# Feed-forward of a two-layer decoder trunk: two of the four weight sums of each seven-product step made by accumulating transfers, the others in place, with plain half steps between the products

## The chip, the cores and the metric

One core of a Trainium2 chip runs the whole program. The metric is the device time of one execution in microseconds. Below, PE is the matrix engine, PEld its weight loads, DVE the vector engine, ACT the scalar engine, POOL the GpSimd engine, and SP the engine that issues the transfers.

## The reference

A trunk of two layers over 256 tokens of width 2048, all in 32-bit floats. Layer 0 mixes by a gated position-wise block beside cross-attention into 256 memory tokens; layer 1 mixes by multi-head latent attention beside the same kind of cross-attention. What matters here is the channel mixer that ends each layer, with D_FF = 5632:

```
def swiglu_ffn(h, w_gate, w_up, w_down):
    return (jax.nn.silu(h @ w_gate) * (h @ w_up)) @ w_down

h = h + rms_norm(mix, norm_gains[i, 1])
f = swiglu_ffn(rms_norm(h, norm_gains[i, 2]), ffn_w_gate[i], ffn_w_up[i], ffn_w_down[i])
h = h + rms_norm(f, norm_gains[i, 3])
```

## The kernel before

**Number format.** Each 32-bit operand is split into two parts of a shorter format, `hi` and `lo`, and a product becomes three matmuls: hi by hi, hi by lo, lo by hi (`mm3`, L212 to L214). Activations are split once and kept. Weights are streamed: a transfer of the SP queue brings them into a staging tile `wst` (three in a ring), ACT casts to `whi` (L166 in `split`, L179 in `wsplit`), DVE subtracts to get `wlo` (L167, L181). `whi` and `wlo` are rings of four, so a split may run at most four groups of matmuls ahead of PE.

**The feed-forward.** The weights of gate and up lie interleaved, 256 columns of gate and then 256 of up. `ffn` goes through the hidden columns in five parts (`parts`), of 2, 2, 2, 2 and 3 chunks of 1024 columns. After each part `to_tokens` multiplies what the part made by the rows of `w_down` that belong to it. The first part is all plain matmuls. In parts two to five, so in nine chunks of a layer and 18 in all, a chunk has four steps `g`, each over a quarter of the 16 feature tiles, and a step has two halves:

- `seven_step` on one half of the chunk's columns treats tokens, features and gate/up as 2 by 2 blocks and makes seven block products in the place of eight. It needs the four loaded weight blocks (b11 and b21 are gate, b12 and b22 are up), and four sums of them. Its products go to four PSUM banks, the set `seven`.
- `plain_step` on the other half makes the ordinary products in 512-column matmuls, 24 of them, into two banks of the set `other`.

There are 72 steps. In a step a seven-product half has 7 products of 2 tiles by 3 matmuls, 42 matmuls of 256 columns.

**The sums before.** `stage` loads both halves with two 512 KB transfers each into `wst` tiles. In `seven_step` DVE makes two sums at once (L504, 1024 columns, reading `wst` and writing a separate tile `ws`), then the third (L508) and the fourth (L510), 512 columns each. ACT and DVE split the pair b11, b21, the pair of sums one and three, the pair two and four, and b22 alone. After the last step of a chunk `seven_hidden` puts the seven products together and applies the gate, while the plain half of that step is still to come; then `hidden` does the same for the plain half.

**What sets the order.** The code emits instructions in program order, small background pieces (`tick`, `to_features`) in between; a scheduler then fixes one static order for every engine's queue from tiles, buffers and its own estimates. On the chip each queue runs strictly in that order. Nothing runs on POOL in the feed-forward.

Of the kernel before, what the change touches and what calls it, by code (L numbers as in the profile page):

```python
# [10 lines left out]
F32 = mybir.dt.float32  # L11
# [6 lines left out]
P = 128  # L18
# [30 lines left out]
def trunk(ctx, tc, x, mem, positions, norm_gains, w_mem_kv, w_down, a_w_in, a_b_s, a_w_out, w_kv_a, w_uk, w_uv,  # L49
# [352 lines left out]
    def ffn(i, xp, r, R, gcol, each, hp, need):  # L402
# [66 lines left out]
        def stage(col, g):  # L469

            st = wtile().rearrange("p (h k n) -> p h k n", h=2, k=2)
            rows = w_gate_up[i].rearrange("(h k p) n -> p h k n", h=2, p=P)
            for e in range(2):
                sp.dma_start(out=st[:, e], in_=rows[:, e, 2 * g:2 * g + 2, col:col + 512])
            return st

        def parts_of_sum(src, n=1024):
            hi = wpool.tile([P, 1024], F32R, tag="whi", name="whi", bufs=4)
            lo = wpool.tile([P, 1024], F32R, tag="wlo", name="wlo", bufs=4)
            hv, lv = hi[:, :n], lo[:, :n]  # L480
            if len(src.shape) == 4:
                hv, lv = [t.rearrange("p (h k n) -> p h k n", h=2, k=2) for t in (hv, lv)]
            elif len(src.shape) == 3:
                hv, lv = [t.rearrange("p (k n) -> p k n", k=2) for t in (hv, lv)]
            split(hv, lv, src)
            return hi, lo

        def seven_step(col, g, X):
            st = stage(col, g)
            room = tmp.tile([P, D], F32, tag="gb", name="ws", bufs=2)  # L490
            t13, t24 = room[:, :1024], room[:, 1024:]
            b11, b21, b22 = st[:, 0, :, :S], st[:, 1, :, :S], st[:, 1, :, S:]
            sums = room.rearrange("p (s k n) -> p s k n", s=4, k=2)
# [21 lines left out]

        def seven_hidden(X, f):

            m1, m2, m5, m6 = X[0][:, :S], X[0][:, S:], X[1][:, S:], X[3][:, :S]
            v = tmp.tile([P, 512], F32, tag="lat", name="v", bufs=2)
            act.copy(out=v[:, :S], in_=m1)  # L520
            dve.tensor_tensor(out=v[:, S:], in0=m6, in1=v[:, :S], op=ALU.add)
            u = tmp.tile([P, 512], F32, tag="lat", name="u", bufs=2)
            dve.tensor_tensor(out=u.rearrange("p (x n) -> p x n", x=2), in0=X[1].rearrange("p (x n) -> p x n", x=2),
                              in1=v[:, S:].rearrange("p (o n) -> p o n", o=1).broadcast_to([P, 2, S]), op=ALU.add)
            dve.tensor_tensor(out=m1, in0=m2, in1=v[:, :S], op=ALU.add)
            sg = tmp.tile([P, 512], F32, tag="sg", name="sg")
            act.activation(out=sg[:, :S], in_=m1, func=AF.Silu)
            dve.tensor_tensor(out=X[2], in0=X[2], in1=u, op=ALU.add)
            act.activation(out=sg[:, S:], in_=X[2][:, :S], func=AF.Silu)
# [29 lines left out]
        for pi, (c0, ncn) in enumerate(parts):  # L559
# [572 lines left out]
```

## Time and profile before

| | |
|---|---|
| median of 3 runs | 2120.69 us (2119.86 to 2126.76) |
| profiled execution | 2121.68 us, span of the trace 2120.0 us |
| PE, PEld | 2094.3 us busy (99%), 1835.1 us (87%) |
| DVE, ACT, POOL | 1568.0 us (74%), 1119.4 us (53%), 4.1 us (0%) |
| granted PE clock | 0.998 of full |
| DMA | 397.05 MB on SP's queue, 188 GB/s over the span |
| weight transfers of the feed-forward, up and gate | 288 of 512 KB, 4.5 us from issue to landing (median) |

Busy shares are averages over stages with different limits; the stretches of the trace in which seven-product steps run are eight, one for each part but the first of either layer. A row that says "idle 1.19 <-ACT whi L166" means that the engine stood idle 1.19 us before this instruction and that the ACT instruction at L166 which writes `whi` ended the wait. Matmuls overlap in the record, so their rate is read from the distance of their starts.

### The profile page before, as it was taken

Reading aid. Unit: us, or ns where it says so; the run is one execution under the profiler, and the core shown is the slowest. Engines: PE = TensorE matmul, PEld = TensorE weight load, DVE = VectorE, ACT = ScalarE, POOL = GpSimd, SP = SyncE. Lnnn points to the kernel's source line nnn. Section 1 sums busy time; section 2 is a strip of 40 time slices with the busy share of each in tenths; the row PEclk is TensorE's granted clock in tenths of the full one; section 3 lists DMA queues with packets and bytes.
Section 4 is the critical chain, followed back from the end, with each engine's and each line's share of the span. In section 5 each row is a group of like instructions: output and inputs, shape, how many; then the busy total and the mean of one; then the engine's idle time right before and its main releaser. Section 6 shows DMA issues by size and latency. Waiting matters only on the chain.

```text
span 2120.0 us, 30041 instructions
## 1 busy us (share of the span) xinstructions
PE 2094.3 (99%) x11922; PEld 1835.1 (87%) x11922; DVE 1568.0 (74%) x2151; ACT 1119.4 (53%) x1478; POOL 4.1 (0%) x11
## 2 busy tenths in 40 slices
PE   8999999999999999999999999999999999999998
PEld 7889989788888888889889998978888888889987
DVE  6556755976868878689767775597686877868966
ACT  6544444655545545455545654565554554545543
POOL 0000000000000000000000000000000000000000
PEclk9999999999999999999999999999999999999999
DMA  9655365555565655655754534555556565565563
GB/s 359 250 181 174 92 221 185 178 181 177 195 202 179 201 179 186 209 178 199 242 176 136 181 122 140 183 174 189 177 190 200 178 218 179 189 207 168 199 222 130
DMA packets 153981, 398.96 MB, mean 188 GB/s; under 512 B 9456, under 2 KB 16880, under 8 KB 152816
## 3 DMA queue, kind: packets, MB, share of 16 engines
q1 hardware_dynamic: 153840, 397.05, 56.4%
q8 instruction: 93, 1.52, 0.3%
q14 instruction: 48, 0.39, 0.1%
HBM read 394.91 MB, written 2.10 MB: 187 GB/s over the span
## 4 chain that ended last, share of the span: by engine, by line
PE 91%; DVE 5%; DMA 2%; ACT 1%; issue 1%; SPq 0%; DVEq 0%; ACTq 0%
PE bank L214 29%; PE bank L213 29%; PE bank L212 29%; DMA wst<-in_w_gate_up 2%; PE bank L418 1%; DVE wlo L181 1%; DVE wlo L187 1%; DVE h L362 1%; PE bank L240 0%; PE bank L1016 0%; PE bank L1017 0%; DVE ws L504 0%; PE bank L707 0%; PE bank L1041 0%; DVE wlo L167 0%
## 5 line engine op out<-in xcount | busy, mean ns | idle before, releaser
L212 PE MATMUL bank<-whi,hl 128*128 128x512 f32 (+3 forms) x2880 | 1030.8, 359 | 0.9 <-ACT hl L166 0.7
L213 PE MATMUL bank<-wlo,hl 128*128 128x512 f32 (+3 forms) x2880 | 1026.6, 356 | 3.6 <-DVE wlo L181 1.9
L214 PE MATMUL bank<-whi,hl 128*128 128x512 f32 (+3 forms) x2880 | 1025.5, 356 | 0.0
L181 DVE TENSOR_TENSOR wlo<-wst,whi 128x1024 fp32r<-128x1024 f32 (+1 forms) x398 | 468.8, 1183 | 237.5 <-ACT whi L179 236.2
L213 PEld LDWEIGHTS bank<-wlo,hl 128*128 128x128 f32 x2880 | 542.3, 188 | 82.1 <-DVE wlo L181 4.1
L214 PEld LDWEIGHTS bank<-whi,hl 128*128 128x128 f32 x2880 | 542.3, 188 | 77.6 <-DVE hl L167 0.5
L212 PEld LDWEIGHTS bank<-whi,hl 128*128 128x128 f32 x2880 | 542.5, 188 | 76.2 <-ACT hl L166 1.9
L179 ACT CAST whi<-wst 128x1024 fp32r<-128x1024 f32 (+1 forms) x398 | 405.0, 1020 | 381.2 <-PE bank L214 346.3
L187 DVE SCALAR_TENSOR_TENSOR wlo<-wst,gains,whi 128x1024 fp32r<-128x1024 f32 (+3 forms) x216 | 255.7, 1193 | 131.0 <-ACT whi L185 128.1
L185 ACT ACTIVATE whi<-wst,gains 128x1024 fp32r<-128x1024 f32 (+3 forms) x216 | 232.2, 1080 | 216.7 <-PE bank L214 131.2
L166 ACT CAST whi<-ws 128x1024 fp32r<-128x1024 f32 x144 | 151.1, 1049 | 159.0 <-PE bank L214 81.0
L167 DVE TENSOR_TENSOR wlo<-ws,whi 128x1024 fp32r<-128x1024 f32 x144 | 175.6, 1220 | 57.0 <-ACT whi L166 56.8
L166 ACT CAST whi<-wst 128x1024 fp32r<-128x1024 f32 (+1 forms) x144 | 120.3, 835 | 108.1 <-PE bank L214 107.3
L167 DVE TENSOR_TENSOR wlo<-wst,whi 128x1024 fp32r<-128x1024 f32 (+1 forms) x144 | 137.0, 951 | 22.0 <-ACT whi L166 22.0
L212 PE MATMUL bank<-hl,whi 128*128 128x256 f32 x448 | 129.1, 288 | 7.0 <-ACT whi L185 7.0
L214 PE MATMUL bank<-hl,wlo 128*128 128x256 f32 x448 | 127.1, 285 | 1.0 <-DVE wlo L187 1.0
L213 PE MATMUL bank<-hl,whi 128*128 128x256 f32 x448 | 127.1, 284 | 0.0
L504 DVE TENSOR_TENSOR ws<-wst 128x1024 f32<-128x1024 f32 x72 | 88.0, 1223 | 26.1 <-DMA wst<-in_w_gate_up 25.7
L212 PEld LDWEIGHTS bank<-hl,whi 128*128 128x128 f32 x448 | 85.2, 190 | 10.2 <-ACT whi L185 7.0
L213 PEld LDWEIGHTS bank<-hl,whi 128*128 128x128 f32 x448 | 85.2, 190 | 2.8
L214 PEld LDWEIGHTS bank<-hl,wlo 128*128 128x128 f32 x448 | 84.8, 190 | 1.5 <-DVE wlo L187 1.4
L213 PE MATMUL bank<-wlo,sx 128*128 128x256 f32 x288 | 81.2, 282 | 0.0
(206 smaller groups left out, 1549.7 us busy)
## 6 DMA issues: line engine op xcount, KB each, us to landing
wst<-in_w_gate_up SPq DMA_DIRECT2D x288, 512.0 KB, 4.5
wst<-in_ffn_w_down SPq DMA_DIRECT2D x76, 1024.0 KB, 5.1
wst<-in_w_gate_up SPq DMA_DIRECT2D x32, 1024.0 KB, 4.9
wst<-in_a_w_in SPq DMA_DIRECT2D x24, 1024.0 KB, 5.1
wst<-in_w_mem_kv SPq DMA_DIRECT2D x15, 1024.0 KB, 6.5
wst<-in_ffn_w_down SPq DMA_DIRECT2D x12, 768.0 KB, 4.5
wst<-in_a_w_out SPq DMA_DIRECT2D x8, 1024.0 KB, 6.0
wst<-in_b_w_in SPq DMA_DIRECT2D x8, 1024.0 KB, 4.9
```

What stands on the lines that cost most here:

```text
L166: ins = act.copy(out=hi, in_=src)
L167: dve.tensor_tensor(out=lo, in0=src, in1=hi.bitcast(F32), op=ALU.subtract)
L179: act.copy(out=hi[:, :n], in_=src)
L181: dve.tensor_tensor(out=lo[:, :n], in0=src, in1=hi[:, :n].bitcast(F32), op=ALU.subtract)
L185: act.activation(out=hi[:, :n], in_=src, func=AF.Copy, scale=g)
L187: dve.scalar_tensor_tensor(out=lo[:, :n], in0=src, scalar=g, in1=hi[:, :n].bitcast(F32), op0=ALU.mult, op1=ALU.subtract)
L212: pe.matmul(out=o, lhsT=a[0], rhs=b[0], start=start, stop=False, **kw)
L213: pe.matmul(out=o, lhsT=a[0], rhs=b[1], start=False, stop=False, **kw)
L214: line["pe"] = pe.matmul(out=o, lhsT=a[1], rhs=b[0], start=False, stop=stop, **kw).ins
L362: ins = dve.scalar_tensor_tensor(out=h[:, b, cs], in0=yv, scalar=rs[b], in1=h[:, b, cs], op0=ALU.mult, op1=ALU.add)
L418: pe.transpose(out=pt[:, q, b, :], in_=hv[:, b * S + q * P:b * S + (q + 1) * P], identity=ident)
L504: dve.tensor_tensor(out=sums[:, 0:2], in0=st[:, :, :, S:], in1=st[:, 0].rearrange("p k (x n) -> p x k n", x=2), op=ALU.add)
```

## The change

The step's own weights get a tile of their own, `ws`, of four blocks q0 to q3 (256 KB each; the ring of two that held the sums before). SP loads b11, b21, b22 and once more b11 into q0 to q3, 256 columns wide each. Two sums are made by transfers that POOL issues and that add what they read to what lies in SBUF: b12 onto q3 as soon as b11 has landed there, and b12 onto q2 (which holds b22) once b22 has been split. DVE makes the other two in place: q0 = q2 + q0, then q1 = q0 + q1. The products are put into four groups in another order, and the two plain halves of a step stand ahead of the first and between the second and the third. The plain half now takes the first 512 columns of a chunk and the seven products the second, so `seven_hidden` comes last in a chunk.

```
-        def stage(col, g):
-
-            st = wtile().rearrange("p (h k n) -> p h k n", h=2, k=2)
-            rows = w_gate_up[i].rearrange("(h k p) n -> p h k n", h=2, p=P)
-            for e in range(2):
-                sp.dma_start(out=st[:, e], in_=rows[:, e, 2 * g:2 * g + 2, col:col + 512])
-            return st
...
+        def seven_step(col, g, X, between):
+
+            st = tmp.tile([P, D], F32, tag="gb", name="ws", bufs=2)
+            q = st.rearrange("p (q k n) -> p q k n", q=4, k=2)
+            own = rows[:, :, 2 * g:2 * g + 2, :]
+            gate, up = slice(col, col + S), slice(col + S, col + 2 * S)
+            for to, e, c in ((0, 0, gate), (1, 1, gate), (2, 1, up), (3, 0, gate)):
+                sp.dma_start(out=q[:, to], in_=own[:, e, :, c])
+            pool_e.dma_start(out=q[:, 3], in_=own[:, 0, :, up], accum_op=ALU.add)
...
-            wt = parts_of_sum(st[:, :, :, :S])
-            dve.tensor_tensor(out=sums[:, 0:2], in0=st[:, :, :, S:], in1=st[:, 0].rearrange("p k (x n) -> p x k n", x=2),
-                              op=ALU.add)
+            front, back = st[:, :1024], st[:, 1024:]
+            wt = own_split(front)
             products(wt, (xp, 0, 0, X[0][:, :S], True), (xp, 8, 0, X[0][:, S:], False))
-            wt = parts_of_sum(t13)
-            dve.tensor_tensor(out=sums[:, 2], in0=sums[:, 1], in1=b11, op=ALU.add)
-            products(wt, (sz, 0, 0, X[1][:, S:], True), (sx, 0, 0, X[1][:, :S], False))
-            dve.tensor_tensor(out=sums[:, 3], in0=sums[:, 2], in1=b21, op=ALU.add)
-            wt = parts_of_sum(t24)
-            products(wt, (sz, 0, 1, X[3][:, :S], True), (xp, 8, 1, X[2][:, :S], True))
-            wt = parts_of_sum(b22, 512)
-            products(wt, (sx, 0, 1, X[2][:, S:], False))
+            wt = own_split(back[:, :512])
+            products(wt, (sx, 0, 1, X[2][:, S:], True))
+            pool_e.dma_start(out=q[:, 2], in_=own[:, 0, :, up], accum_op=ALU.add)
+            between()
+            dve.tensor_tensor(out=q[:, 0], in0=q[:, 2], in1=q[:, 0], op=ALU.add)
+            wt = own_split(back)
+            products(wt, (sx, 0, 0, X[1][:, :S], True), (sz, 0, 0, X[1][:, S:], False))
+            dve.tensor_tensor(out=q[:, 1], in0=q[:, 0], in1=q[:, 1], op=ALU.add)
+            wt = own_split(front)
+            products(wt, (sz, 0, 1, X[3][:, :S], True), (xp, 8, 1, X[2][:, :S], False))
...
                     for g in range(4):
-                        seven_step(col, g, seven)
-                        if g == 3:
-                            behind_done()
-                            seven_hidden(seven, c * 4)
-                        plain_step(col + 512, g, other[:2])
+                        plain = plain_steps(col, g, other[:2])
+                        next(plain)
+
+                        def between():
+                            next(plain)
+                            if g == 3:
+                                behind_done()
+                                hidden(other[:2], c * 4, False)
+
+                        seven_step(col + 512, g, seven, between)
                     behind_done()
-                    hidden(other[:2], c * 4 + 2, False)
+                    seven_hidden(seven, c * 4 + 2)
```

`own_split` splits as before (L166 and L167 in `split`). `seven_hidden` does the same arithmetic with its results in SBUF in the place of PSUM. Lines of the new code are named by the rows that follow: L486 SP's loads of `ws`, L487 and L502 the two accumulating transfers, L504 and L507 the two sums, L536 the plain half's loads.

How DVE's queue stands within a chunk before, from one L504 on: the sums of a step stand with the splits of the step ahead of it, and wait for nothing but loads that were issued earlier and for DVE itself.

```order
L504 TENSOR_TENSOR ws_5209<-wst_5206 128x1024 [waits DMAHW5_49,DMAHW4_49]
L181 TENSOR_TENSOR wlo_5175<-wst_5171,whi_5174 128x1024 [waits DMAHW2_49,Activation_49]
L508 TENSOR_TENSOR ws_5209<-ws_5209,wst_5206 128x512 [waits DVE_49]
L181 TENSOR_TENSOR wlo_5191<-wst_5171,whi_5190 128x1024 [waits DMAHW3_49,Activation_49]
L167 TENSOR_TENSOR wlo_5211<-wst_5206,whi_5210 128x1024 [waits Activation_49]
L167 TENSOR_TENSOR wlo_5228<-ws_5209,whi_5227 128x1024 [waits Activation_49]
L510 TENSOR_TENSOR ws_5209<-ws_5209,wst_5206 128x512 [waits DVE_49]
L167 TENSOR_TENSOR wlo_5246<-ws_5209,whi_5245 128x1024 [waits Activation_49]
L167 TENSOR_TENSOR wlo_5262<-wst_5206,whi_5261 128x512 [waits Activation_49]
```

And in the change, the same queue through one step within a chunk (`ws_5857` is the step's tile, `ws_5959` the next step's; DMASW are the transfers that POOL issues): the split of b22 (128x512), one plain split, the two sums, the splits of the two pairs of sums, then the next step's plain half, its first pair and its b22. The 1024-column sum is gone; L504 now waits for the accumulating transfer onto q2, and six instructions stand between it and the next split of b22.

```order
L167 TENSOR_TENSOR wlo_5880<-ws_5857,whi_5879 128x512 [waits DMAHW2_49,Activation_49]
L181 TENSOR_TENSOR wlo_5891<-wst_5838,whi_5890 128x1024 [waits DMAHW5_49,Activation_49]
L504 TENSOR_TENSOR ws_5857<-ws_5857 128x512 [waits DMASW5_49,DVE_49]
L507 TENSOR_TENSOR ws_5857<-ws_5857 128x512 [waits DVE_49]
L167 TENSOR_TENSOR wlo_5908<-ws_5857,whi_5907 128x1024 [waits DMASW4_49,Activation_49]
L167 TENSOR_TENSOR wlo_5925<-ws_5857,whi_5924 128x1024 [waits Activation_49]
L181 TENSOR_TENSOR wlo_5944<-wst_5940,whi_5943 128x1024 [waits DMAHW6_49,Activation_49]
L167 TENSOR_TENSOR wlo_5966<-ws_5959,whi_5965 128x1024 [waits DMAHW7_49,DMAHW6_49,Activation_49]
L167 TENSOR_TENSOR wlo_5982<-ws_5959,whi_5981 128x512 [waits DMAHW0_49,Activation_49]
```

POOL's queue in the same place, empty before: two accumulating transfers a step in turn. L502 of a step waits for DVE's split of b22; L487, onto q3 of the next step, waits for SP's load into q3 and stands behind that L502.

```order
L487 DMA ws_5857<-in_w_gate_up 128x2x256 [waits DMAHW3_49,DMASW2_49,DMASW0_49]
L502 DMA ws_5857<-in_w_gate_up 128x2x256 [waits DMAHW2_49,DVE_49]
L487 DMA ws_5959<-in_w_gate_up 128x2x256 [waits DMAHW1_49,DMASW3_49,DMASW1_49]
L502 DMA ws_5959<-in_w_gate_up 128x2x256 [waits DMAHW0_49,DVE_49]
L487 DMA ws_6093<-in_w_gate_up 128x2x256 [waits DMAHW7_49,DMASW5_49,DMASW4_49]
```

At the border of two chunks in the change, DVE's queue from the first step's split of b22 on, where the chunk ahead of it has just ended: what `hidden`, `seven_hidden` and `to_features` (`hl`) add stands partly between b22's split and L504, partly behind L504.

```order
L167 TENSOR_TENSOR wlo_6116<-ws_6093,whi_6115 128x512 [waits DMAHW6_49,Activation_49]
L167 TENSOR_TENSOR hl01_73<-bank4_80,hl00_72 128x512 [waits Activation_49]
L517 TENSOR_TENSOR v_6054<-bank7_83,v_6054 128x256 [waits PE_49]
L518 TENSOR_TENSOR v_6054<-bank2_78,v_6054 128x256 [waits DVE_49]
L520 TENSOR_TENSOR u_6055<-bank3_79,v_6054 128x512
L181 TENSOR_TENSOR wlo_6127<-wst_6068,whi_6126 128x1024 [waits Activation_49]
L522 TENSOR_TENSOR v_6054<-bank3_79,u_6055 128x256 [waits DVE_49]
L504 TENSOR_TENSOR ws_6093<-ws_6093 128x512 [waits DMASW1_49]
L523 TENSOR_TENSOR u_6055<-bank6_82,u_6055 128x512 [waits DVE_49,PE_49]
L167 TENSOR_TENSOR wlo_6144<-ws_6093,whi_6143 128x1024 [waits DMASW0_49,Activation_49]
L528 SCALAR_TENSOR_TENSOR hv_6065<-u_6055,sg_6056 128x256 [waits DVE_49]
L528 SCALAR_TENSOR_TENSOR hv_6065<-v_6054,sg_6056 128x256 [waits Activation_49]
```

Two more of `hidden` (L434) stand ahead of the first row, and the second sum and another `hl` behind the last. In before the four PSUM banks that `seven_hidden` reads were free again one plain half step ahead of a part's end; now `seven_hidden` is the last thing of a part, and the first chunk of `to_tokens` writes the same four banks.

## Rows read from the trace of the kernel before

**Rows 1.** The page: busy time of each engine over the span

```profile
span 2120.0 us, 30041 instructions
...
PE 2094.3 (99%) x11922; PEld 1835.1 (87%) x11922; DVE 1568.0 (74%) x2151; ACT 1119.4 (53%) x1478; POOL 4.1 (0%) x11
...
PEclk9999999999999999999999999999999999999999
```

**Rows 2.** Windows: the eight seven-product stretches; length, engines' busy us, clock, DMA share, GB/s

```profile
497.00:590.00 93.00, 92.72 (x556) 81.73 (x555) 76.99 (x85) 51.33 (x61) 0.00 (x0) 1.00 0.56 182
...
762.00:854.00 92.00, 92.00 (x551) 80.97 (x550) 78.50 (x88) 48.90 (x56) 0.00 (x0) 1.00 0.55 183
...
sum 822.00, PE 820.10 PEld 725.83 DVE 703.70 ACT 446.81 POOL 0.00; mean PE 102.51 PEld 90.73 DVE 87.96 ACT 55.85 POOL 0.00
```

**Rows 3.** Waits of PE, whole span: us in total, times, longest

```profile
PE bank L212 <- ACT whi L185: 7.0, 1, 7.0
PE bank L213 <- DVE wlo L181: 1.9, 2, 1.3
```

**Rows 4.** Timeline of PE, one step: plain half, then seven products; start us, us

```profile
704.42 0.39 PE L212 MATMUL bank<-whi,hl 128*128 128x512 f32 x1
...
709.99 0.28 PE L212 MATMUL bank<-whi,hl 128*128 128x256 f32 x1
...
714.98 0.39 PE L212 MATMUL bank<-whi,hl 128*128 128x512 f32 x1
```

**Rows 5.** Timeline of DVE, part of one step

```profile
578.32 0.69 DVE L167 TENSOR_TENSOR wlo<-wst,whi 128x512 fp32r<-128x512 f32 x1
578.92 1.22 DVE L504 TENSOR_TENSOR ws<-wst 128x1024 f32<-128x1024 f32 x1
...
582.93 1.22 DVE L167 TENSOR_TENSOR wlo<-wst,whi 128x1024 fp32r<-128x1024 f32 x1
584.07 1.22 DVE L167 TENSOR_TENSOR wlo<-ws,whi 128x1024 fp32r<-128x1024 f32 x1
```

**Rows 6.** Groups by form, 497 to 1028 us (36 steps): busy us, mean ns, idle before

```profile
L504 DVE TENSOR_TENSOR ws<-wst 128x1024 f32<-128x1024 f32 x36 | 44.0, 1222 | 14.0 <-DMA wst<-in_w_gate_up 13.8
...
L510 DVE TENSOR_TENSOR ws<-ws,wst 128x512 f32<-128x512 f32 x36 | 24.6, 685 | 0.3
L508 DVE TENSOR_TENSOR ws<-ws,wst 128x512 f32<-128x512 f32 x36 | 24.6, 685 | 0.2
...
L418 PE MATMUL bank<-ident,hv 128*128 128x128 f32 x64 | 11.1, 276 | 0.2 <-DVE hv L534 0.2
L167 DVE TENSOR_TENSOR hl<-bank,hl 128x512 fp32r<-128x512 f32 x16 | 10.9, 683 | 0.3 <-ACT hl L166 0.3
...
L434 DVE TENSOR_TENSOR hv<-bank,sg 128x256 f32<-128x256 f32 x16 | 6.5, 417 | 1.4 <-ACT sg L433 1.3
...
L534 DVE SCALAR_TENSOR_TENSOR hv<-bank,sg 128x256 f32<-128x256 f32 x16 | 6.0, 412 | 0.0
L528 DVE TENSOR_TENSOR bank<-bank,u 128x512 f32<-128x512 f32 x8 | 5.5, 689 | 0.0
...
L525 DVE TENSOR_TENSOR bank<-bank,v 128x256 f32<-128x256 f32 x8 | 3.4, 428 | 1.3 <-ACT v L520 1.3
...
L521 DVE TENSOR_TENSOR v<-bank,v 128x256 f32<-128x256 f32 x8 | 3.3, 416 | 0.0
...
L520 ACT COPY v<-bank 128x256 f32<-128x256 f32 x8 | 3.0, 373 | 6.2 <-PE bank L214 6.2
```

**Rows 7.** Tile `wst`, SP's issues, 500 to 960 us: issue ns min/median/max; time to landing

```profile
L474 SPq DMA_DIRECT2D wst<-in_w_gate_up x118: 367/410/1152, 503.4 to 957.4; - x118
...
DMA to landing us min/median/max: 3.5/4.5/6.7
```

**Rows 8.** DMA issues, whole span: KB each, median us from issue to landing

```profile
wst<-in_w_gate_up SPq DMA_DIRECT2D x288, 512.0 KB, 4.5
...
wst<-in_ffn_w_down SPq DMA_DIRECT2D x6, 512.0 KB, 3.6
...
out<-h SPq DMA_DIRECT2D x8, 256.0 KB, 2.2
```

More of the change, by code (lines that the diff above doesn't have):

```diff
@@ L467, in normalise, with own_split @@
             yield
-        def stage(col, g):
-            st = wtile().rearrange("p (h k n) -> p h k n", h=2, k=2)
-            rows = w_gate_up[i].rearrange("(h k p) n -> p h k n", h=2, p=P)
-            for e in range(2):
-                sp.dma_start(out=st[:, e], in_=rows[:, e, 2 * g:2 * g + 2, col:col + 512])
-            return st
-        def parts_of_sum(src, n=1024):
+        rows = w_gate_up[i].rearrange("(h k p) n -> p h k n", h=2, p=P)
+        def own_split(src):
             hi = wpool.tile([P, 1024], F32R, tag="whi", name="whi", bufs=4)
             lo = wpool.tile([P, 1024], F32R, tag="wlo", name="wlo", bufs=4)
[L480 to L485, printed above, removed]
-            return hi, lo
[L488 to L493, printed above, removed]
+            n = src.shape[-1]
+            split(hi[:, :n], lo[:, :n], src)
+            return hi, lo
+        def seven_step(col, g, X, between):
[6 more added lines that the diff above has]
+            pool_e.dma_start(out=q[:, 3], in_=own[:, 0, :, up], accum_op=ALU.add)
             def products(wt, *what):
@@ L516, in seven_hidden @@
+            between()
[5 more added lines that the diff above has]
+            products(wt, (sz, 0, 1, X[3][:, :S], True), (xp, 8, 1, X[2][:, :S], False))
         def seven_hidden(X, f):
-            m1, m2, m5, m6 = X[0][:, :S], X[0][:, S:], X[1][:, S:], X[3][:, :S]
@@ L519, in seven_hidden @@
             v = tmp.tile([P, 512], F32, tag="lat", name="v", bufs=2)
-            act.copy(out=v[:, :S], in_=m1)
-            dve.tensor_tensor(out=v[:, S:], in0=m6, in1=v[:, :S], op=ALU.add)
             u = tmp.tile([P, 512], F32, tag="lat", name="u", bufs=2)
+            sg = tmp.tile([P, 512], F32, tag="sg", name="sg")
+            act.copy(out=v[:, :S], in_=X[0][:, :S])
+            dve.tensor_tensor(out=v[:, S:], in0=X[3][:, :S], in1=v[:, :S], op=ALU.add)
+            dve.tensor_tensor(out=v[:, :S], in0=X[0][:, S:], in1=v[:, :S], op=ALU.add)
@@ L523, in seven_hidden @@
+            act.activation(out=sg[:, :S], in_=v[:, :S], func=AF.Silu)
             dve.tensor_tensor(out=u.rearrange("p (x n) -> p x n", x=2), in0=X[1].rearrange("p (x n) -> p x n", x=2),
                               in1=v[:, S:].rearrange("p (o n) -> p o n", o=1).broadcast_to([P, 2, S]), op=ALU.add)
-            dve.tensor_tensor(out=m1, in0=m2, in1=v[:, :S], op=ALU.add)
-            sg = tmp.tile([P, 512], F32, tag="sg", name="sg")
-            act.activation(out=sg[:, :S], in_=m1, func=AF.Silu)
@@ L528, in seven_hidden @@
-            dve.tensor_tensor(out=X[2], in0=X[2], in1=u, op=ALU.add)
-            act.activation(out=sg[:, S:], in_=X[2][:, :S], func=AF.Silu)
-            dve.tensor_tensor(out=m5, in0=m5, in1=u[:, :S], op=ALU.add)
+            dve.tensor_tensor(out=v[:, S:], in0=X[1][:, S:], in1=u[:, :S], op=ALU.add)
+            dve.tensor_tensor(out=u, in0=X[2], in1=u, op=ALU.add)
+            act.activation(out=sg[:, S:], in_=u[:, :S], func=AF.Silu)
             hv = tmp.tile([P, 512], F32, tag="hv", name="hv")
-            for b, o in enumerate((X[2][:, S:], m5)):
+            for b, o in enumerate((u[:, S:], v[:, S:])):
@@ L536, in seven_hidden, with plain_steps @@
             bg.append(behind_group[-1])
-        def plain_step(col, g, banks):
-            st = stage(col, g)
+        def plain_steps(col, g, banks):
+            st = wtile().rearrange("p (h k n) -> p h k n", h=2, k=2)
+            for e in range(2):
+                sp.dma_start(out=st[:, e], in_=rows[:, e, 2 * g:2 * g + 2, col:col + 512])
             for e in range(2):
@@ L547, in plain_step @@
                 tick()
+                yield
         early = list(range(4)) + list(range(8, 12)) + list(range(4, 8)) + list(range(12, 16))
```

## The prediction

> **What bounds the kernel now.** I read the page's busy times first: PE is busy for 99% of the span at the full granted clock, DVE for 74% and ACT for 53% [rows 1]. A share over the whole span does not tell what the changed stage is worth, so I cut out the eight stretches in which seven-product steps run. They are 822.0 us together, and PE is busy for 820.10 of them; DVE is busy for 703.70 of them, 86% [rows 2]. So in the stage that the change touches, PE waits for next to nothing: 1.9 us in all. The longest wait of PE in the whole program is 7.0 us, at the start, for a first split that the change does not touch; the next entry, for a weight split, is 1.9 us in two waits [rows 3]. The reader should take from these three views that what DVE does there is hidden behind PE, with a margin of about a seventh.
>
> Then the timeline gives the beat. A plain half step starts at 704.42 and the seven products behind it at 709.99, the next plain half at 714.98 [rows 4]: 5.57 us for 24 wide matmuls, 4.99 for 42 narrow ones, **10.56 us a step**. The change keeps the number and the shapes of these matmuls, so this beat is a floor for it.
>
> **The change, part by part.**
>
> *The 1024-column sum that DVE no longer makes.* 72 instructions of 1.222 us [rows 6], 88 us of DVE. The two other sums stay, in place, at the same 512 columns and 0.685 us each [rows 6]; the splits are the same in number and width. All 88 us lie beside PE's work. PE's idle time in the stretches bounds what can come of it: at most 1.9 us [rows 2]. I put it at nothing.
>
> *The loads.* SP now issues six transfers a step in the place of four, four of them of 256 KB. An issue takes SP 0.41 us [rows 7], so 2.5 us of 10.56: hidden. The `ws` tile of a step is loaded when the last split of the step two before it is done; its first split comes about a step later, some 10 us, against 4.5 us to landing, 6.7 at worst [rows 7]. That the rows are now 1 KB long costs little, as far as the trace tells: the transfers of `w_down` with rows of 1 KB land 512 KB in 3.6 us [rows 8]. Nothing for the loads.
>
> *The accumulating transfer onto q3 (L487).* It is due when the pair q2, q3 is split, more than a step after its tile was free. Hidden, even at the slowest landing of rows 7 twice over.
>
> *The accumulating transfer onto q2 (L502).* This is the term that decides. It cannot be issued before DVE has split b22, since it overwrites b22, and DVE's L504 waits for it. The order shows what DVE may do in between: one plain split. DVE's queue is strict, so behind the waiting L504 stand L507, the two splits of sums, and the next step's plain split, first pair and b22; and the next L502 waits for the last of these. That is a ring: transfer, six instructions and a b22 split of DVE, transfer. I price DVE's share of it from the distance of starts in its timeline: a 1024-column instruction 1.14 us (582.93 to 584.07), a 512-column one 0.60 (578.32 to 578.92) and 0.69 until it is done [rows 5]. Two sums of 0.60, four splits of 1.14 and the b22 split of 0.69 make **6.45 us**. The casts of ACT fit beside them. So the step takes the longer of 10.56 and 6.45 + L, where L is the time from the end of the b22 split to the landing of the transfer. **The transfer is free up to L = 4.1 us; beyond that every microsecond of L costs 72 us.** It is not PE's 99% that decides here but how deep the queue behind one wait is.
>
> No row shows a transfer that POOL issues, nor one that adds. The bounds of L: below, the quickest transfer of 256 KB, `out`, 2.2 us when nearly nothing else moves [rows 8], and 0.5 for the hand-over and the issue (an issue takes SP 0.41 [rows 7]), 2.7. Above, the slowest landing of a weight load in these stretches, 6.7 [rows 7], and 0.5, so 7.2. I take the median of the 512 KB loads in the same stretches, 4.5 us [rows 7]: the accumulating transfer brings 256 KB, has to read 256 KB that lie in SBUF as well, and falls among the next step's loads. With 0.5 for the hand-over, **L = 5.0**, 0.9 over what is free: 72 x 0.9 = 65 us.
>
> The Trainium skill, DMA: Bandwidth & Descriptors, section Specifications, gives about 1 us to the first byte where GpSimd makes the descriptors and about 0.6 where SP's hardware does. An estimate from that page would lengthen L by the 0.4 us between them and bring 29 us more, 2249; no run here shows it, and my sum goes without it.
>
> *The ends of chunks.* Once DVE's ring is what binds, what else DVE does at a chunk's end counts too, as far as it stands outside the wait for L502. By the order that is two L434 (0.417 each), one 512-column addition of `seven_hidden` (0.689), two closing multiplications (0.412 each) and one `hl` split (0.683) [rows 6]: 3.0 us a chunk. PE's own work at a chunk's end, the transposes, 11.1 us for the eight chunks in the window [rows 6], 1.4 each, is in the time of before already. 18 x (3.0 - 1.4) = 29 us. With L under 4.1 it costs nothing, since the margin of four steps takes it up.
>
> *The ends of parts.* `seven_hidden` is now last, and the first chunk of `to_tokens` writes the banks that it reads. PE may wait for ACT's copy (0.373) and two additions of DVE (0.416 and 0.428) before the first bank is free [rows 6], 1.2 us, at eight part ends: 0 to 10 us. I take the middle, 5.
>
> Sum, against the profiled execution of 2121.68 us: 65 + 29 + 5 = 99, so 2221; the median of the runs shown is 1 us lower, and I write **2220 us**, 4.7% slower.
>
> **The rivals.**
>
> *The transfer is hidden.* If L stays under 4.1 us, the plain half step between the products covers it, DVE is only relieved, and the time is that of before with part of the term at the parts' ends, 2122 us. For it: 2.2 us for the same bytes in `out`, which would make L 2.7 [rows 8], and DMA engines that are busy for only 55% of the stretch [rows 2]. Against it: that transfer ran at the end of the program, alone; in the stretches not one weight load landed in under 3.5 us [rows 7], and 3.5 with 0.5 is already at the edge. 15%. The Trainium skill, DMA: Bandwidth & Descriptors, section Anatomy of one DMA, has a rule by which this rival would be the outcome: about 2.0 us and the bytes at 436 GB/s, an estimate of 2.6 us for 256 KB. By the same rule a load of 512 KB would take 3.2 us; the trace has 4.5 [rows 7], so the rule is short of what this load of the engines makes.
>
> *The adding is slow at the DMA engines themselves.* The engines are busy for 55% of a stretch with 2 MB a step [rows 2]. The change reads 2.5 MB and re-reads 0.5 MB; at the same price by the byte that is 83%, still below full. If the half megabyte that is added costs four times its bytes, it is 110%, the loads queue up as well, and L is 8 us or more: 72 x 3.9 + 34 = 315, 2436 us. What speaks for it is that no row shows an adding transfer; against it, that 256 KB is a small part of the traffic. 12%.
>
> *DVE's relief shows.* The stretches hold 1.9 us of idle PE [rows 2]; the whole span 26 (2120.0 less 2094.3 [rows 1]), most of it at the start and in stages that the change leaves alone. 2118 at best, and more than 0.3% only if PE's own beat gets faster, for which no row speaks. 3%.
>
> **How the numbers follow.** The forecast, a wait that DVE's ring cannot hide with L between 4.1 and 6.6 us, gets 70%. About 0.3%, 6 us, is what a measurement of this kernel can tell from no change. Slower by more: the forecast and the slow adding, 82%. Within: 15%. Faster: 3%. The range reaches down to 2119, so that it takes in the hidden transfer, and up to L = 6.6 with the other two terms, 2121.68 + 180 + 34 = 2335; outside lie the slow adding and the relief, 15%.
>
> **What would show it.** Right: in the rows of L504 an idle time of DVE ended by the transfer onto `ws`, in nearly every step, of L less about 1.2 us; PE idle before the group of the two sums, ended by the split of `ws`; a step of 11.5 us from one plain half to the next; DVE busy some 80 us less. POOL's issues have L502 landing 4 to 5 us after issue. Wrong: L504 waits, but PE does not, and the step is still 10.6 us (the ring is looser than I counted, or L is short); or PE waits in the first split of a step (the loads are late, not the sum); or the loss lies at the eight part ends alone.

## The result, and the profile after

The changed kernel takes 2349.55 us (median of 4 runs, 2345.10 to 2357.03) beside 2121.59 for the kernel before in the same session: ratio 1.108, 95% interval 1.1055 to 1.1105. It is 228 us slower, where 99 was forecast and 2335 was the upper end of the range. Times of different runs are compared below by their ratios to the kernel before, since the kernel before itself came out between 2117.8 and 2121.6 from session to session. One of the four runs of an experiment below (e6_beside) took 2473.39 us at a granted clock of 0.798 and is left out of its time and ratio.

The profiled execution has a span of 2355.3 us. The page's busy times and the granted clock by slice, to be held against [rows 1]:

```profile
PE 2177.2 (92%) x11922; PEld 1886.5 (80%) x11922; DVE 1500.2 (64%) x2079; ACT 1114.7 (47%) x1478; POOL 177.8 (8%) x155
...
PEclk9999999999899998999999999999989899999989
```

PE executes the same 11922 matmuls and is now idle for 178 us where it was idle for 26. DVE is busy for 68 us less (its instructions last 86 us less in sum, and those that follow each other closely overlap in the record). PE's busy time has grown by 83 us, and the clock row has eights where before there were none: the same matmuls run slower in places.

The eight stretches with seven-product steps, first, last and the sum, in the view of busy times by window (length, busy time of each engine with its instructions, PE's granted clock, DMA share, GB/s), to be held against [rows 2]:

```profile
503.00:616.00 113.00, 97.20 (x545) 83.85 (x543) 65.88 (x74) 48.69 (x59) 18.08 (x15) 0.94 0.69 181
...
2101.00:2269.00 168.00, 143.18 (x817) 124.02 (x815) 105.02 (x122) 72.29 (x86) 26.53 (x22) 0.94 0.72 184
sum 1006.00, PE 866.95 PEld 749.19 DVE 613.91 ACT 429.92 POOL 161.55; mean PE 108.37 PEld 93.65 DVE 76.74 ACT 53.74 POOL 20.19
```

They are 1006 us together where they were 822. PE is idle in 139 of them where it was idle in 1.9. The DMA engines are busy for about 0.7 of the stretch, not for 0.55, and move no more per second than before. The waits say for what (engine, line, what ended the wait: us in total, times, longest):

```profile
POOL ws L502 <- DVE wlo L167: 745.1, 71, 43.4
...
ACT whi L166 <- DMA ws<-in_w_gate_up: 380.8, 69, 10.9
DVE ws L504 <- DMA ws<-in_w_gate_up: 310.4, 72, 9.7
...
POOL ws L487 <- issue: 287.5, 56, 9.2
```

and the groups and the DMA issues of the page (KB each, median us from issue to landing) bring the price:

```profile
L504 DVE TENSOR_TENSOR ws<-ws 128x512 f32<-128x512 f32 x72 | 49.8, 692 | 310.4 <-DMA ws<-in_w_gate_up 310.4
...
L502 POOL DMA_DIRECT2D ws<-in_w_gate_up x72 | 87.2, 1212 | 751.7 <-DVE wlo L167 745.1
...
wst<-in_ffn_w_down SPq DMA_DIRECT2D x76, 1024.0 KB, 6.3
ws<-in_w_gate_up SPq DMA_DIRECT2D x288, 256.0 KB, 4.2
wst<-in_w_gate_up SPq DMA_DIRECT2D x144, 512.0 KB, 4.9
ws<-in_w_gate_up POOLq DMA_DIRECT2D x144, 256.0 KB, 5.1
```

All 72 L504 wait for the adding transfer, and all but one L502 wait for the split of b22: the ring of the prediction is there. That it reaches PE is in PE's own waits. These two are the longest in total, and both stand before the first matmuls of the group of the two sums, right behind the plain half between the products:

```profile
PE bank L212 <- ACT whi L166: 89.8, 27, 5.6
PE bank L213 <- DVE wlo L167: 31.4, 35, 1.1
```

What the prediction lacked is in the figures above: L502 lands 5.1 us after issue in the median, but L504 waits up to 9.7. The instruction itself holds POOL for 1.21 us, where an issue of SP takes 0.41 [rows 7].

From the trace I took for each step the time L from the end of b22's split to the start of L504, and the distance from one L504 to the next (64 distances within a part; the shortest is 11.9 us, over PE's 10.56, and the median is 13.0). L is 6.61 us on average (median 5.61): 0.44 until L502 starts, 6.09 until it lands, 0.08 until L504 starts. A distance less its L is 6.71 us in the median; the prediction had 6.45 for this share of DVE. The long L come in certain steps. Two steps in a row, GpSimd's queue, SP's, and DVE:

```profile
562.80 1.22 POOL L502 DMA_DIRECT2D ws<-in_w_gate_up  x1 [6.46 <-DVE wlo L167]
...
577.11 1.22 POOL L502 DMA_DIRECT2D ws<-in_w_gate_up  x1 [8.33 <-DVE wlo L167]
```

```profile
565.54 0.88 SPq L536 DMA_DIRECT2D wst<-in_w_gate_up  x2
...
577.86 0.37 SPq L202 DMA_DIRECT2D wst<-in_ffn_w_down  x1
```

```profile
567.29 0.69 DVE L504 TENSOR_TENSOR ws<-ws 128x512 f32<-128x512 f32 x1 [1.44 <-DMA ws<-in_w_gate_up]
...
574.88 1.82 DVE L167 TENSOR_TENSOR wlo<-ws,whi 128x1024 fp32r<-128x1024 f32 x2
576.62 1.22 DVE L181 TENSOR_TENSOR wlo<-wst,whi 128x1024 fp32r<-128x1024 f32 x1
...
586.75 0.69 DVE L504 TENSOR_TENSOR ws<-ws 128x512 f32<-128x512 f32 x1 [8.91 <-DMA ws<-in_w_gate_up]
```

In the first step SP's next load is issued 2.74 us after L502, and the sum starts 4.5 us after L502. In the second the two splits at 574.88, the pair and b22, end at 576.70 and release L502; the plain split behind them ends at 577.84 and releases a 1 MB load of `w_down`. That is issued 0.75 us after L502, while POOL's 1.22 us are still running, and the sum starts 9.6 us after L502. Over the whole trace: in 25 of the 72 steps a load of the plain half or of `w_down` is issued less than 1 us after L502, and there L502 lands in 8.21 us on average (6.18 to 10.06), in 24 of the 25 within 0.5 us of that load's own landing; in the 47 others in 4.96.

### The profile page after: what moved, and what is told of

Same layout as the page of the kernel before. It is cut to its first block, busy times and chain, and to the rows that moved or that the text cites. A ratio compares the mean times of both kernels' runs of the same rounds, so it can differ in the third digit from the quotient of the medians.

```text
span 2355.3 us, 30697 instructions
## 1 busy us (share of the span) xinstructions
PE 2177.2 (92%) x11922; PEld 1886.5 (80%) x11922; DVE 1500.2 (64%) x2079; ACT 1114.7 (47%) x1478; POOL 177.8 (8%) x155
## 3 DMA queue, kind: packets, MB, share of 16 engines
q0 software_dynamic: 39168, 37.76, 11.7%
## 4 chain that ended last, share of the span: by engine, by line
PE 52%; DMA 18%; DVE 14%; issue 11%; ACT 4%; SPq 0%; POOL 0%; DVEq 0%; ACTq 0%; POOLq 0%
DMA ws<-in_w_gate_up 18%; PE bank L212 16%; PE bank L213 16%; PE bank L214 16%; DVE wlo L167 5%; DVE wlo L181 3%; ACT whi L166 2%; DVE ws L504 2%; DVE ws L507 1%; ACT whi L179 1%; PE bank L418 1%; DVE wlo L187 1%; DVE h L362 0%; PE bank L240 0%; PE bank L1019 0%
## 5 line engine op out<-in xcount | busy, mean ns | idle before, releaser
L181 DVE TENSOR_TENSOR wlo<-wst,whi 128x1024 fp32r<-128x1024 f32 (+1 forms) x398 | 470.6, 1185 | 303.6 <-ACT whi L179 301.7
L212 PEld LDWEIGHTS bank<-whi,hl 128*128 128x128 f32 x2880 | 560.7, 195 | 85.0 <-DVE v L518 6.3
L214 PEld LDWEIGHTS bank<-whi,hl 128*128 128x128 f32 x2880 | 559.8, 194 | 76.9 <-DVE hl L167 0.5
L179 ACT CAST whi<-wst 128x1024 fp32r<-128x1024 f32 (+1 forms) x398 | 405.0, 1019 | 392.8 <-PE bank L214 380.9
L166 ACT CAST whi<-ws 128x1024 fp32r<-128x1024 f32 (+1 forms) x288 | 267.5, 942 | 477.4 <-DMA ws<-in_w_gate_up 380.8
L167 DVE TENSOR_TENSOR wlo<-ws,whi 128x1024 fp32r<-128x1024 f32 (+1 forms) x288 | 307.7, 1087 | 29.2 <-ACT whi L166 25.7
L504 DVE TENSOR_TENSOR ws<-ws 128x512 f32<-128x512 f32 x72 | 49.8, 692 | 310.4 <-DMA ws<-in_w_gate_up 310.4
L212 PE MATMUL bank<-whi,sx 128*128 128x256 f32 x288 | 89.5, 311 | 99.0 <-ACT whi L166 89.8
L487 POOL DMA_DIRECT2D ws<-in_w_gate_up x72 | 86.5, 1202 | 1120.3 <-DVE hl L167 716.5
L212 PEld LDWEIGHTS bank<-whi,sx 128*128 128x128 f32 x288 | 58.3, 202 | 116.7 <-ACT whi L166 101.3
L502 POOL DMA_DIRECT2D ws<-in_w_gate_up x72 | 87.2, 1212 | 751.7 <-DVE wlo L167 745.1
L213 PEld LDWEIGHTS bank<-wlo,sx 128*128 128x128 f32 x288 | 59.2, 206 | 44.4 <-DVE wlo L167 42.9
```

The costliest lines, as they stand in the source:

```text
L166: ins = act.copy(out=hi, in_=src)
L167: dve.tensor_tensor(out=lo, in0=src, in1=hi.bitcast(F32), op=ALU.subtract)
L179: act.copy(out=hi[:, :n], in_=src)
L181: dve.tensor_tensor(out=lo[:, :n], in0=src, in1=hi[:, :n].bitcast(F32), op=ALU.subtract)
L212: pe.matmul(out=o, lhsT=a[0], rhs=b[0], start=start, stop=False, **kw)
L213: pe.matmul(out=o, lhsT=a[0], rhs=b[1], start=False, stop=False, **kw)
```

## The experiments

Two accounts had to be told apart. By the first, L502's landing stands in a ring of DVE and each microsecond of it is paid 72 times; the question is then why it is 6.1 and not 4.5. By the second, adding transfers clog the DMA engines for everybody, waited for or not. Beside them stood the fallen clock and the part ends.

**The wait taken away, both adding transfers kept (e1_early_add).**

```
+            b22 = tmp.tile([P, 512], F32, tag="sg", name="b22")
+            sp.dma_start(out=b22.rearrange("p (k n) -> p k n", k=2), in_=own[:, 1, :, up])
+            for to in (3, 2):
+                pool_e.dma_start(out=q[:, to], in_=own[:, 0, :, up], accum_op=ALU.add)
...
+            wt = own_split(b22)
```

> The changed kernel, but b22 is loaded twice, once into a small tile of its own from which it is split, so that both sums are made by adding transfers ahead of time and L502's wait for the split of b22 is gone; two adding transfers a step stay, and SP loads 0.25 MB a step more. Theory 1 (the ring: DVE waits in every step for a transfer that cannot start before b22 is split): no ring, DVE has 8 us of work in 10.56, the time goes back to 2120 to 2140 us. Rival 2 (the adding transfers slow the DMA engines for everything): the same two transfers run, so it stays above 2250 us. Rival 3 (the new order of the half steps and the ends of parts): it stays near 2350 us.

2198.09 us, ratio 1.0373 (1.0358 to 1.0389). The waits of POOL tell where the rest sits:

```profile
POOL ws L490 <- issue: 579.3, 117, 10.9
```

POOL waits 117 times for nothing that the profile shows. In the trace, 131 of the 143 adding transfers of this run start 0.26 to 0.5 us after the one before has landed, and none earlier, although none of these 131 waits for the semaphore of the one before. So **adding transfers go one at a time**: two a step take 12.0 us in the median, from the first one's start to the second one's landing, and that is longer than 10.56. The steps follow each other at 11.9 us in the median.

**No adding transfer (e4_dve_all).** The order, the tile and the placing of the change stay; SP loads b12 into q3, and DVE makes both sums.

```
-            pool_e.dma_start(out=q[:, 2], in_=own[:, 0, :, up], accum_op=ALU.add)
+            dve.tensor_tensor(out=q[:, 2], in0=q[:, 2], in1=q[:, 3], op=ALU.add)
+            dve.tensor_tensor(out=q[:, 3], in0=q[:, 3], in1=q[:, 0], op=ALU.add)
```

> The changed kernel with its order of half steps, its tile and its sums in place, but no transfer of POOL: SP loads b12 into q3, DVE adds q3 onto q2 and then q0 onto q3. Theory 1 (the ring through L502): 2120 to 2140 us, and DVE at 9.2 us of work a step again. Rival 2 (adding transfers slow the DMA engines): 2120 to 2140 us as well. Rival 3 (the order of the half steps, the ends of parts): it stays above 2250 us. What is left over the time of before here is the price of the order alone.

2134.68 us, ratio 1.0074 (1.0057 to 1.0091). By the ratios (1.1080 less 1.0074), 213 of the 228 us hang on the adding transfers. The sums of DVE are hidden, as before. PE's waits, the part ends in the first row:

```profile
PE bank L212 <- DVE v L518: 12.6, 8, 1.6
...
PE bank L212 <- ACT whi L179: 4.0, 10, 0.4
```

**The transfer in the ring without adding (e3_pool_plain).** L502 overwrites b22 with b12.

```
-            pool_e.dma_start(out=q[:, 2], in_=own[:, 0, :, up], accum_op=ALU.add)
+            pool_e.dma_start(out=q[:, 2], in_=own[:, 0, :, up])
```

> The changed kernel, only that the transfer onto q2 (L502) does not add: POOL issues it in the same place and b12 overwrites b22, so the sum b22 + b12 is left out. Theory 1 with the length of the wait set by POOL's issue of 1.2 us and by the loads that run beside it: the same waits, L 5.3 us in most steps and 8 to 10 in three of eight, 2320 to 2350 us. If the adding itself is what makes the wait long: L some 4 us and 2180 to 2230 us.

2227.65 us, ratio 1.0514 (1.0493 to 1.0536). The landing, minimum, median and maximum, by the view of line L502, and its issue (ns):

```profile
L502 POOL DMA_DIRECT2D ws<-in_w_gate_up x72: 737/738/762, 510.1 to 2136.1; - x72
...
DMA to landing us min/median/max: 3.1/3.7/6.8
```

against the changed kernel:

```profile
L502 POOL DMA_DIRECT2D ws<-in_w_gate_up x72: 1195/1211/1224, 509.3 to 2256.6; - x72
...
DMA to landing us min/median/max: 4.4/5.1/10.1
```

Adding costs 1.4 us of landing in the median, 0.47 of them in POOL's issue, and L falls from 6.61 to 4.63. The slow landings remain without adding, and in the same place: the 17 transfers with a load issued less than 1 us behind them take 5.96 us on average, the 55 others 3.6. But a plain transfer does not stay until the load has landed: in these 17 the load lands 2.2 us behind it in the median.

**The same, issued by SP (e5_sp_plain).**

```
+            sp.dma_start(out=q[:, 2], in_=own[:, 0, :, up])
```

> The changed kernel, but the second transfer (L502) is issued by SyncE and overwrites instead of adding; the sum b22 + b12 is left out. The dependency split, transfer, difference, split stays as it is. Theory that the ring has its length from the adding transfer on GpSimd's queue: the transfer takes 4.2 to 4.5 us as SyncE's other 256 KB loads do, the step falls to 10.6 to 11.2 us, time 2140 to 2190 (with GpSimd's plain transfer it was 2228). Rival, any transfer in that place costs as much, because SyncE's queue is held while the load waits for the split: 2220 or more, and the weight loads behind it land late.

2171.71 us, ratio 1.0245 (1.0221 to 1.0269), and L is 3.82 us. The same two rows:

```profile
L502 SPq DMA_DIRECT2D ws<-in_w_gate_up x72: 367/368/422, 509.4 to 2075.7; - x72
...
DMA to landing us min/median/max: 2.6/3.6/5.8
```
The ring has its length from POOL and from the adding; 57 us lie between this and the plain transfer of POOL, 120 between that and the adding one (ratio differences of 0.0269 and 0.0566). The 57 are not the price of POOL's issue alone: on SP's queue only 3 of the 72 transfers have a large load issued within 1 us behind them, where there were 17.

**Adding transfers beside the kernel before (e6_beside), and plain ones (e8_beside_pool_plain).** Nobody reads the spare tile.

```
+            sp.dma_start(out=spare, in_=rows[:, 0, 2 * g:2 * g + 2, col:col + S])
+            for _ in range(2):
+                pool_e.dma_start(out=spare, in_=rows[:, 0, 2 * g:2 * g + 2, col + S:col + 2 * S], accum_op=ALU.add)
```

> The kernel before, and beside each seven-product half one more load of 256 KB and two adding transfers of 256 KB by POOL into a tile that nobody reads. Theory 1: nobody waits for them, 2120 to 2135 us. Rival 2 (they slow the DMA engines): weight loads land late, first splits wait, 2180 us or more. Either way the landing of the weight loads (4.5 us in the kernel before) tells by how much the adding transfers hold them up.

> The kernel before with, in each step, one more 256 KB load by SyncE and two 256 KB transfers on GpSimd's queue into a tile that nobody reads, all without adding (with adding on the two it was 2302). Added traffic, nothing left out. Theory that it is the adding that holds up the weight loads (1 KB packets of 101 ns against 46 ns): the weight loads land in 4.4 to 4.7 us, 2115 to 2150. Rival, any transfer on GpSimd's queue or the bytes alone (3.4 MB a step against 2.4) do it: 2230 to 2300.

2298.38 us with adding (ratio 1.0854, 1.0830 to 1.0879), 2149.79 without (1.0141, 1.0124 to 1.0159). That seemed to decide for clogged engines, and it does not. A wait of SP, in the adding run and in the plain one:

```profile
SPq L505 <- DMA spare<-in_w_gate_up: 259.2, 18, 18.1
```

```profile
SPq L505 <- DMA spare<-in_w_gate_up: 104.2, 18, 7.4
```

SP's own load into the spare tile stands in its queue until the adding transfers of the step before are through, which again go one at a time (126 of 143 start within 0.5 us after the landing before; 24 of them the program makes wait for it), and the weight loads stand behind it. I had built a wait into a test of contention: the 155 us between these two waits are about the 149 us between the two times. The loads themselves are held up little: the 512 KB ones land in 4.7 us in the median with adding and 4.5 without, the 1 MB ones of `w_down` in 6.4 and 5.4. What the runs also show is the price at the engines, by the page's DMA queues (packets, MB, share of 16 engines), first with adding in the changed kernel, then plain in e8:

```profile
q0 software_dynamic: 39168, 37.76, 11.7%
```

```profile
q0 software_dynamic: 11520, 37.76, 5.1%
```

For the same 37.76 MB that is 0.117 x 16 x 2355.3 = 4409 us of engine time against 0.051 x 16 x 2145.8 = 1751: 2.5 times. The plain transfers of e8 went in fewer packets, of 4 KB, the adding ones in packets of 1 KB. At the same size, an adding packet takes 102 ns in the median in the changed kernel and a 1 KB packet of SP's loads 46, 2.2 times.

**One adding transfer, early (e2_dve_add).** The sum in q2 is DVE's, from a plain load at the step's start; L487 still adds.

```
+            b12 = tmp.tile([P, 512], F32, tag="sg", name="b12").rearrange("p (k n) -> p k n", k=2)
+            sp.dma_start(out=b12, in_=own[:, 0, :, up])
...
-            pool_e.dma_start(out=q[:, 2], in_=own[:, 0, :, up], accum_op=ALU.add)
+            dve.tensor_tensor(out=q[:, 2], in0=q[:, 2], in1=b12, op=ALU.add)
```

> The changed kernel, but the second sum is taken by VectorE (0.69 us a step more there) from a plain load of b12 into a tile of its own at the step's start; the first sum stays an adding transfer. Same result. No transfer is left in the ring. Theory: ring gone, half of the adding transfers left, so between the kernel with both sums on VectorE (2135) and the one with both adding transfers early (2198): 2150 to 2175. Rival, the adding transfers cost nothing unless waited for: 2130 to 2140.

2137.87 us, ratio 1.0086 (1.0068 to 1.0104), the rival's figure: within what can be told from the run without any adding transfer (1.0074). An adding transfer that nobody waits for, alone in its step, costs nothing that these runs can tell. For one such transfer a step the second account falls, except for the part of it that acts on L502 itself; two a step are too many even early (e1), since they go one at a time.

**The loads kept out of L502's way (e13_loads_wait).** A transfer of 128 bytes into the same tile goes ahead of each load of the plain half and of the first loads of `w_down`, so that the load has to wait for it.

```
+            if i < late:
+                sp.dma_start(out=st[0:1, :, 0:16], in_=ws[0][:1, :32].rearrange("p (k n) -> p k n", k=2))
...
+            sp.dma_start(out=st[0:1, :, 0, 0:16], in_=rows[0:1, :, 2 * g, col:col + 16])
```

> The changed kernel, where each load of the plain half step, and the first three loads of w_down in a part, have a tiny transfer (128 bytes, into the same tile) ahead of them, so that the load itself starts about 2 us later. Same work in the same order on the computing engines. In the changed kernel the 25 of 72 transfers L502 with one of those loads issued less than 1 us after them land in 8.2 us on average, the 47 others in 4.6 to 5.2. Theory that the load overtakes the adding transfer (GpSimd takes 1.2 us to issue it, SyncE 0.4) and that it then waits behind 1 MB: with the load later, all land in 4.5 to 5.5, 25 x 3.3 = 82 us come back, 2250 to 2290. Rival, the length is the adding transfer's own or comes from whatever is moved beside it: landing of the slow ones still 7 us or more, 2330 or more.

2271.73 us, ratio 1.0719 (1.0704 to 1.0734): 77 us come back by making loads later. The adding transfer is L504 in this kernel:

```profile
DMA to landing us min/median/max: 4.4/4.8/6.7
```

The mean is 4.92, that of the undisturbed steps before, and L is 5.43. No large load is issued within 1 us of the adding transfer any more: it was such loads that made the slow landings.

**Filling PE's idle time (e7_filler, e10_filler4).** Matmuls that nobody reads, where PE waits; six a step ahead of the sum in the first, four in the second.

```
+            for _ in range(4):
+                pe.matmul(out=short["banks"][1], lhsT=xp[0][:, 0, :P], rhs=xp[0][:, 0:2, :].rearrange("p k t -> p (k t)"), start=True, stop=True,
+                          skip_group_check=True)
```

> The changed kernel with six more matmuls of 512 columns a step (6 x 0.233 = 1.4 us) that nobody reads, put where TensorE waits for the split: added work, nothing left out. 72 x 1.4 = 101 us of work goes into idle time of TensorE (which is 152 us more than before). Theory that part of the loss is the granted clock falling in long waits (0.964 over the span, busy time 83 us more than before for the same matmuls): the clock comes back to 0.99 or more and the time falls below the changed kernel, to 2290 to 2330. Rival, the clock only follows the idle time and costs nothing of its own: no fall, 2350 to 2400, since the filler is one more thing in the step.

> The changed kernel with four more matmuls of 512 columns a step (4 x 0.233 = 0.93 us, 67 us in all, read by nobody) behind the plain half between the products, where TensorE waits; the order on GpSimd's queue stays that of the changed kernel, unlike with six of them. Added work, nothing left out. Theory that the fallen clock costs time of its own: the clock rises over 0.964 and the time falls to 2300 to 2335. Rival, the ring alone sets the step and TensorE's slower matmuls lie in its idle time, as the filler does: the time stays within 10 us of the changed kernel, 2340 to 2360.

Six gave 2676.37 us (ratio 1.2627, 1.2607 to 1.2647) and told nothing of the clock: the static order came out with the next step's L487 ahead of L502 on POOL, L487 waits there for its own load, and L502 starts 9.2 us after the split in the median. It shows at what price two adding transfers of different steps share one strict queue. Four left POOL's order as it was: 2327.52 us, ratio 1.0988 (1.0967 to 1.1009), clock 0.985 where it was 0.964. The number is the one that I wrote for the clock, yet the reason is not shown: a distance less its L is 6.71 us in the median in the changed kernel and 6.72 here, so PE's slower matmuls do not stand in the ring. What fell is L, from 6.61 to 6.21, with 16 steps in the place of 25 that have a load issued within 1 us of L502. Whether the clock or the filler itself moved the loads stays open.

**The bank sets exchanged (e11_other_banks), and both repairs together (e14_late_banks).**

```
-                seven, other = g4(), g4()
+                other, seven = g4(), g4()
...
+                short["banks"] = seven[:2]
```

> The kernel with both sums on VectorE and no adding transfer (2135), with the two bank sets exchanged, so that the first chunk of the multiplication by w_down writes the set that the plain halves have used and not the one that seven_hidden still reads. Theory that the 16 us left there are the waits for those banks at the eight part ends (12.6 us for VectorE's additions and 4.0 for ACT's casts in the chain of waits): 2118 to 2125. Rival, they come from the order of the steps (the plain halves between the products) or from the extra sum on VectorE: 2130 to 2137.

> The changed kernel with both repairs found so far: the loads of the plain half and of w_down start about 2 us later (alone: 2272), and the bank sets exchanged so that the first chunk behind a part need not wait for seven_hidden (alone, without adding transfers: 14 us). Theory that the two are separate terms: 2272 - 14 = 2258, range 2250 to 2264, and TensorE's waits for VectorE's additions into u and v (15 us in the run with late loads) are gone. Rival, the part ends cost nothing as long as the ring binds: 2268 to 2275.

On the kernel without adding transfers: 2121.12 us, ratio 1.0008 (0.9999 to 1.0017), the kernel before. The waits for `v` at the part ends are gone, and they were the whole rest there, as far as the interval can tell; the waits for ACT's casts (4.0 us in 10) are still in this run, so they were not the banks. The new order of the step costs nothing that can be told. With the late loads: 2262.96 us, ratio 1.0671 (1.0650 to 1.0692), 10 us less than with late loads alone; of the waits for `u` 8 us stay:

```profile
PE bank L214 <- DVE u L525: 8.1, 8, 2.2
```

No version beat the kernel before; the best of them equals it.

## Why the prediction was wrong in size

- *The floor of PE, and nothing for DVE's relief*: right. The changed order with both sums on DVE and the banks exchanged runs at 1.0008, and DVE, 22 us busier in e11 than before (1589.8 against 1568.0), still does not show.
- *The loads and L487 hidden*: right as far as shown; with L487 alone (e2) the time moves by less than can be told.
- *The ring through L502*: right as a mechanism. DVE's share was put at 6.45 us and measured at 6.71. All 72 L504 wait. The step is 13.0 us in the median where 11.5 was written.
- *L = 5.0*: **the step that failed.** It was taken from the median of SP's plain 512 KB loads, plus 0.5. Measured: 6.61. With that number in the prediction's own formula, 72 x (6.61 - 4.1) = 181 us, and with its 29 us for chunk ends 210, beside 228 measured. This fits better than the formula deserves. In the trace, the 64 distances between L504 and L504 are together 211 us longer than those between the same sums in e11 (L505 there), the same order without an adding transfer; and for these 64, with their L of 6.78 and their ten chunk ends, the formula gives 64 x 2.68 + 16 = 188. It is too low in the other runs too, all the more near the limit, even when it is given all 72 steps: with late loads 72 x 1.33 + 29 = 125 against distances of 130, for L = 4.63 (e3) 67 against 100, for 3.82 (e5) 29 at most against 43. A mean of L hides the steps above the limit, and with 6.71 the limit is 3.9 and not 4.1.
- *What was missing in L* has two parts. POOL's issue of 1.21 us and the adding bring the undisturbed landing to 4.9 and L to 5.43 (e13): 0.43 x 72 = 31 us. The other part, 6.61 - 5.43, is 85 us by the same rule and was 77 in the run: 25 landings of 8.2, where the very next split of DVE releases a large load on SP. SP issues it in a third of the time, and L502 lands only with that load (within 0.5 us of it in 24 of the 25). Why an adding transfer is held so long, and a plain one is not, no run shows. I had bounded L by landings of SP's loads, which have no other queue beside them, and had taken the slow case for an upper end and not for something that the same steps of every part would meet. The range's upper end, L = 6.6, was the mean.
- *Ends of chunks*: 3.0 us of DVE was taken for each, less 1.4 of PE. At a chunk's end two distances less their L are longer than 6.71, 9.41 and 7.45 us in the median at the ten borders inside a part, 3.4 us together: the size of DVE's part was right. What PE's 1.4 takes off was not measured.
- *Ends of parts*: 5 taken, 10 at most. Exchanging the banks gave 14 us without adding transfers (1.0074 to 1.0008) and 10 in the ring. A wait ended by DVE's addition is 1.6 us (12.6 in 8), where I had added 1.2 from durations alone.
- *The slow adding at the engines, priced at four times the bytes and 12%*: measured 2.2 to 2.5 times, and the engines stay at 0.7 of the stretch. The engines are not full, and the large loads land a little later (4.9 us for 4.5, and 6.3 for 5.1 those of `w_down`); it is the one transfer in the ring that is paid for.
- The Trainium skill, DMA: Bandwidth & Descriptors, section Specifications, has about 0.4 us more to the first byte on GpSimd's path. The rows agree in kind: a plain issue holds POOL for 0.74 us where SP takes 0.37, and the plain landings are 4.1 and 3.6 us on average (e3, e5), though 3.7 and 3.6 in the median. By the Trainium skill, DMA: Bandwidth & Descriptors, section Anatomy of one DMA, which is about GpSimd's path, a transfer of 256 KB would be an estimated 2.6 us. The rows differ: the plain one of e3 took at least 3.1, and the adding one never came under 4.4. The prediction had held this rule against a load of SP, which that section is not about.

## What to carry to other kernels

Before moving a sum into a transfer, ask what stands on both sides of it: a transfer that must wait for an engine's instruction and for which that same engine waits makes a ring, and what its latency has over the slack of the ring is paid in every step, whatever the engines' shares. Price that latency in company: look which other queue the same event releases, and which of the two gets its request out first. And of a range for a latency that is paid 72 times, ask for the mean, since the slow cases may come at fixed places.

## What the runs showed of the hardware

- Adding transfers of GpSimd's queue never overlapped: in every run with two a step the next one started 0.26 us or more after the landing of the one before, also where the program had no such wait (102 of the 126 close ones in e6). Plain transfers of the same queue did overlap (90 of 143 in e8, which differs from e6 only in the adding, and 53 in e3).
- An adding transfer of 256 KB holds POOL for 1.21 us (plain: 0.74) and takes 2.2 to 2.5 times the engine time of a plain one; undisturbed it lands in 4.9 us, with a load issued less than 1 us behind it in 8.2.
- After its seven longest waits in the seven-product stretches (5.1 to 5.6 us) PE came back at the lower of its two levels, 1.2 GHz. One of them: it was idle for 5.1 us up to 587.85, and of the two windows behind that the first shows the granted clock (the third figure from the end) at 0.50, the second at full again:

```profile
588.00:594.00 6.00, 5.08 (x22) 4.78 (x23) 5.39 (x6) 3.56 (x4) 0.30 (x2) 0.50 0.68 151
594.00:600.00 6.00, 6.00 (x37) 5.34 (x37) 1.92 (x2) 1.77 (x2) 1.58 (x2) 1.00 0.79 179
```

  PE's 83 us of added busy time go with such stretches (169 us in all at the lower level, 10 before). Their price in the ring was not seen: a distance less its L is 6.71 us in the median where L is over 7 us, and 6.74 where it is shorter.
